# A conv block on one core: ScalarE's tap products and copies moved behind the job's sigmoid, ten VectorE taps moved ahead, the last copies split eight and eight

## The chip, the core and the metric

One NeuronCore of a Trainium2 chip runs the whole kernel. The metric is device time in microseconds (us), the median of several runs. PE is TensorE (PEld its weight loads), DVE is VectorE, ACT is ScalarE, POOL is GpSimd, SP is SyncE, which issues the DMAs.

## The reference

One decoder layer on 256 tokens of width 2048, in float32. A modulation vector comes from `c`; then a convolution mixer; then an MLP:

```python
mod = silu(c) @ mod_w + mod_b                      # sh1, sc1, g1, sh2, sc2, g2
h = rms_norm(x, norm1_g) * (1 + sc1) + sh1
u = h @ w_in + b_in                                # 2048 -> 4096
a, gt = split(u, 2)
u = a * sigmoid(gt)                                # the gate
u = depthwise_causal_conv(u, dw_w, width=31) + dw_b
u = silu(layer_norm(u, ln_g, ln_b))
x = x + (1 + g1) * (u @ w_out + b_out)
h = rms_norm(x, norm2_g) * (1 + sc2) + sh2
x = x + (1 + g2) * (square(relu(h @ w1)) @ w2)     # 2048 -> 8192 -> 2048
```

## The kernel before, in words

Channels lie on the 128 partitions, so a 2048-wide activation is 16 tiles of 128 x 256 tokens. A float32 weight is split into a high half `hi` (a copy by ScalarE, L209) and a low half `lo` (a subtraction, L213, by GpSimd for the input projection), and three matmul products (L234 to L239) stand for one float32 product. Weights arrive by DMA in 1 MB buffers named `raw`, seven of them; a buffer is loaded again when its `lo` has been made.

The change lies in the middle of the kernel. The input projection with its gates is a list of 16 jobs `("in", n)`. The first eight are summed together before 137 us; jobs 8 to 15 follow one after the other, up to about 272 us. Job n computes the two tiles (value and gate half) of channel tile n. Around each job stand, in the order in which the program says them:

- the weight splits of job n+1 (`splits`);
- in jobs 8 to 12 `shared_taps`: tile 7 is convolved by ScalarE and GpSimd together. ScalarE makes 2 or 7 products of a shifted tile with a tap's weight (L700, L703), GpSimd adds them up (L705);
- `copy_wide`: sixteen small copies (32 partitions x 284) that lay a gated tile out for a convolution on TensorE (L779 on ScalarE, L777 on DVE). `COPY_AT` says at which job which tile is copied;
- the job's matmuls;
- the evacuation: `evac` (L536 on ScalarE, L537 on DVE) adds the two halves of the sum, `gate` makes the sigmoid (L817, ScalarE) and the gated product `u` (L819, DVE);
- for seven tiles the convolution on TensorE itself (`pe_conv`, matmuls of L802), evacuated by ScalarE (L810); then modulation rows (matmuls of L328), which fill TensorE's time;
- `advance(n)`: a number of taps (L676, one 128 x 256 multiply-add each) of the eight tiles that DVE convolves, 31 taps a tile, joined by L679. `ADVANCE` says how many taps follow the gate of which job.

Behind the tiles 0 and 1 a mean is found (L428 on TensorE, L737), and subtracted from the convolved tiles as a shift (L741, on GpSimd L855); sums and sums of squares follow by L747 (squares by L480, L946). Job 15's gate is the last one: its tile 15 is copied at once, by DVE and ScalarE together, and convolved on TensorE, and layer norm, SiLU and the output projection hang on it.

A scheduler puts each engine's instructions in order by the order of the program and by priority: `urgent()` moves what stands in it ahead by 400 places, and `issue_after(x)` keeps an instruction behind `x`. Within an engine the order is then fixed. PSUM tiles named `mm` exist twice; jobs and TensorE convolutions take them in turn, so a matmul may have to wait for an evacuation two tiles before it.

Of the kernel before, what the change touches and what calls it, by code (L numbers as in the profile page):

```python
# [11 lines left out]
ALU = mybir.AluOpType  # L12
# [5 lines left out]
KT = D // P  # L18
# [25 lines left out]
CONV_AT = {9: (0,), 10: (1,), 11: (9,), 12: (10,), 14: (12,), 15: (14,)}  # L44
POOL_TILE = 7
POOL_TAPS = {8: 2, 9: 7, 10: 7, 11: 7, 12: 7}
ADVANCE = {7: 41, 8: 10, 9: 45, 10: 45, 11: 38, 12: 24, 13: 24, 14: 99}
SHIFT = 2
COPY_AT = {8: 0, 9: 1, 10: 9, 11: 10, 13: 12}
PADDING = 752  # L50
# [6 lines left out]
HELD = 8  # L57
# [11 lines left out]
def conv_block(ctx: ExitStack, tc: tile.TileContext, x, vec, dwq, c_row, mod_r, mod_c, w_first, w_in, w_out, w1, w2, out):  # L69
    nc = tc.nc  # L70
# [15 lines left out]
    def col(name, j=0, n=1):  # L86
        at = VEC[name] + j
        return v[:, at : at + n]
# [31 lines left out]
    state = {"used": 0}  # L120
# [12 lines left out]
    def urgent():  # L133
        return tc.high_priority(offset=URGENT)
# [315 lines left out]
    def two():  # L450
        return tmp.tile([P, 2, T], F32, name="two", bufs=6)
# [44 lines left out]
    for job in jobs:  # L496
        n = quota.get(job, 0)
# [3 lines left out]
        if job[:2] in LATE_GATE:  # L501
            n = LATE_GATE[job[:2]][job[2]]
# [22 lines left out]
    def splits(job):  # L525
        for c in range(2):
            if job + (c,) in parts_early:
                continue
            on_pool = job[0] == "in" or job in POOLED
            with urgent():  # L530
                split_w(job + (c,), nc.gpsimd if on_pool else nc.vector)

    def evac(p, cs=slice(0, 2), out=None):
        t1 = two()[:, cs, :]
        t2 = two()[:, cs, :] if out is None else out
        nc.scalar.activation(t1, p[:, cs, T : 2 * T], AF.Copy)  # L536
        nc.vector.tensor_tensor(t2, p[:, cs, 0:T], t1, op=ALU.add)  # L537
        return t2
# [4 lines left out]
    for k2 in range(HALF):  # L543
# [5 lines left out]
        for j in range(2):  # L549
            g = (2 * k2 + j) % 4  # L550
# [68 lines left out]
    for k in range(KT):  # L619
# [4 lines left out]
        if c == 0:  # L624
            n = two()
# [30 lines left out]
    def cv(k):  # L656
        return cvs[k // 4][:, k % 4, :]
# [6 lines left out]
    def tap_of(ct, j):  # L664
        return u[ct][:, j : j + T], col("dww", ct * TAPS + j)
# [27 lines left out]
    def shared_taps(n):  # L693
        at, total = POOL_TILE, cv(POOL_TILE)
        slots = [cvs[3][:, m, :] for m in range(4)] + [cv(11)]
        slots += [cp.tile([P, T], F32, name="part", bufs=2) for _ in range(n - len(slots))]
        with urgent(), tc.issue_after(state["w_hi"]), tc.issue_after(state["pool"]):
            if n == POOL_TAPS[HELD]:
                s, w = tap_of(at, 0)
                nc.scalar.activation(total, s, AF.Identity, scale=w, bias=col("dwb", at))  # L700
            for part in slots[:n]:
                s, w = tap_of(at, next(taken_taps))
                state["part"] = nc.scalar.activation(part, s, AF.Copy, scale=w).ins  # L703
            for part in slots[:n]:
                state["part_sum"] = nc.gpsimd.tensor_tensor(total, total, part, op=ALU.add).ins  # L705
# [21 lines left out]
    def advance(n):  # L727
        for _ in range(n):
            next(conv_taps, None)
# [9 lines left out]
    def add_shift(tiles, n):  # L739
        by = state["small"][:, None, T : 2 * T].to_broadcast([P, n, T])  # L740
        return nc.vector.tensor_tensor(tiles, tiles, by, op=ALU.add).ins  # L741
# [28 lines left out]
    def copy_wide(ct, both=True):  # L770
        wides[ct] = cp.tile([P, 4, T + 28], F32, name="wide", bufs=2)
        for q in range(4):
            for g in range(4):
                dst = wides[ct][32 * q : 32 * q + 32, g, :]
                src = u[ct][32 * g : 32 * g + 32, q : q + T + 28]
                if both and (g % 2 or (q, g) == (3, 2)):
                    nc.vector.tensor_copy(dst, src)  # L777
                else:
                    nc.scalar.activation(dst, src, AF.Copy)  # L779
# [35 lines left out]
    def gate(i, t2):  # L815
        sg = two()[:, 0, :]
        state["sg"] = nc.scalar.activation(sg, t2[:, 1, :], AF.Sigmoid, bias=col("b_in", KT + i))  # L817
        u[i] = ubufs[i % len(ubufs)]
        state["gated"] = nc.vector.scalar_tensor_tensor(  # L819
            u[i][:, PAD : PAD + T], t2[:, 0, :], col("b_in", i), sg, op0=ALU.add, op1=ALU.mult  # L820
        ).ins
        return sg
# [6 lines left out]
    with urgent():  # L829
# [10 lines left out]
        gate(7, held[7])  # L840
    advance(ADVANCE[HELD - 1])

    for n, job in enumerate(jobs):
# [5 lines left out]
            taken = [(key, take(key)) for key in cols_in]  # L849
        if n < len(jobs) - 1:  # L850
            splits(jobs[n + 1])
        if n in POOL_TAPS:
            shared_taps(POOL_TAPS[n])
        if n == KT - 3:
            nc.gpsimd.tensor_tensor(cv(POOL_TILE), cv(POOL_TILE), state["shift"], op=ALU.add)  # L855
        if n in COPY_AT:
            with tc.issue_after(state["sg"].ins) if n == HELD else ExitStack():
                copy_wide(COPY_AT[n], False)
        if n == KT - 1:
            for key in parts_early:  # L860
# [43 lines left out]
        if kind == "in":  # L904
            with urgent():
                gate(i, evac(p, out=p[:, :, 0:T]) if i < KT - 1 else p[:, :, 0:T])
                if i >= KT - 2:
                    copy_wide(i, i == KT - 1)
            if n == KT - 4:
                add_shift(cvs[0], 4)  # L910
                add_shift(cvs[1][:, 0:3, :], 3)
# [15 lines left out]
            with tc.issue_after(state["gated"]):  # L927
                advance(ADVANCE.get(n, 0))
            if n == KT - 2:
# [162 lines left out]
        else:  # L1092
# [13 lines left out]
            for t, cs, p in sums.pop((kind, i // 2)):  # L1106
# [9 lines left out]
                else:  # L1116
                    g = two().rearrange("p a t -> p (a t)")[:, cs]
# [62 lines left out]
```

## Time and profile before

| | |
|---|---|
| time, median of 3 runs | 1098.15 us (1098.1 to 1098.56) |
| the profiled execution's own time | 1097.87 us |
| its span | 1096.1 us, 15367 instructions |
| granted TensorE clock | 0.997 |
| busy over the span | PE 1078.0 us (98%), DVE 747.5 (68%), ACT 520.2 (47%), POOL 217.2 (20%) |
| moved by DMA | 314.20 MB, mean 287 GB/s |

The span runs from the first to the last instruction of the trace; the time has a little more around it. A row of a timeline gives start and length in us, the engine, the line, what is written and read, and in brackets the idle time ahead of it with what ended it; "x16" merges sixteen instructions. One matmul instruction can show as several records, so their number is not that of the program's matmuls.

### The profile page before, as it was taken

To read this page: it belongs to the slowest core of one execution; us is meant where nothing else is said; L and a number is where in the kernel's file an instruction comes from. 1 tells how busy PE (TensorE), PEld (TensorE's weight loads), DVE (VectorE), ACT (ScalarE), POOL (GpSimd) and SP (SyncE) were. 2 spreads that over 40 slices of the span, in tenths; PEclk is the share of its full clock that TensorE was granted. 3 is DMA by queue.
4 is the path that set the end of the run, shared out by engine and by line. 5 is a ranking of instruction groups with operands and counts; after the bars stand their busy time and mean duration, and the time that the engine had idled before them with its cause. 6 is when DMAs were issued, how large, how long until landed. Compare 5 with 4: busy or idle time off the path is not lost.

```text
span 1096.1 us, 15367 instructions
## 1 busy us (share of the span) xinstructions
PE 1078.0 (98%) x5970; PEld 890.6 (81%) x5970; DVE 747.5 (68%) x1020; ACT 520.2 (47%) x705; POOL 217.2 (20%) x149
## 2 busy tenths in 40 slices
PE   6999999999999999999999999999999999999998
PEld 3888875778599988888888888888888888888887
DVE  5777889978667877787855677545566665565653
ACT  4111398666685686444444444333444333444431
POOL 0000179979589261000000000000000000000000
PEclk8999999999999999999999999999999999999999
DMA  9999998985999967899977899657887877788611
GB/s 382 420 421 420 414 416 304 375 331 227 381 397 399 369 261 242 267 314 346 399 272 202 246 262 317 240 133 296 251 240 236 227 213 213 232 247 238 213 66 39
DMA packets 142314, 314.20 MB, mean 287 GB/s; under 512 B 87585, under 2 KB 105505, under 8 KB 107297
## 3 DMA queue, kind: packets, MB, share of 16 engines
q1 hardware_dynamic: 142096, 313.10, 81.2%
q8 instruction: 47, 0.77, 0.3%
q14 instruction: 25, 0.20, 0.1%
q10 hardware_dynamic: 146, 0.13, 0.0%
HBM read 301.13 MB, written 12.07 MB: 286 GB/s over the span
## 4 chain that ended last, share of the span: by engine, by line
PE 82%; DMA 10%; ACT 3%; DVE 3%; issue 1%; DVEq 0%; SPq 0%
PE mm L276 20%; PE mm L275 20%; PE mm L277 20%; DMA raw<-mod_c 7%; PE mm L238 5%; PE acc L235 2%; PE acc L234 2%; PE acc L236 2%; PE mm L239 2%; DMA first<-w_first 2%; PE row L328 1%; DVE raw L408 1%; PE mm L802 1%; ACT wide L779 1%; DMA raw<-w_in 1%; ACT hi L209 1%
## 5 line engine op out<-in xcount | busy, mean ns | idle before, releaser
L209 ACT ACTIVATE hi<-raw 128x1024 fp32r<-128x1024 f32 x320 | 335.7, 1058 | 361.5 <-PE mm L277 330.2
L213 DVE TENSOR_TENSOR lo<-raw,hi 128x1024 fp32r<-128x1024 f32 x257 | 312.3, 1220 | 182.8 <-ACT hi L209 179.2
L276 PE MATMUL mm<-lo,u 128*128 128x512 f32 x496 | 193.0, 389 | 0.0
L275 PE MATMUL mm<-hi,u 128*128 128x512 f32 x496 | 193.0, 389 | 0.0
L277 PE MATMUL mm<-hi,u 128*128 128x512 f32 x496 | 192.9, 389 | 0.0
L277 PE MATMUL mm<-hi,hl 128*128 128x512 f32 x480 | 186.7, 389 | 0.0
L276 PE MATMUL mm<-lo,hl 128*128 128x512 f32 x480 | 186.7, 389 | 0.0
L275 PE MATMUL mm<-hi,hl 128*128 128x512 f32 x480 | 186.7, 389 | 0.0
L213 POOL TENSOR_TENSOR lo<-raw,hi 128x1024 fp32r<-128x1024 f32 x63 | 156.1, 2508 | 37.0 <-ACT hi L209 37.0
L408 DVE SCALAR_TENSOR_TENSOR raw<-raw,cond 128x2048 f32<-128x2048 f32 x50 | 118.0, 2362 | 38.0 <-DMA raw<-mod_c 38.0
L277 PEld LDWEIGHTS mm<-hi,u 128*128 128x128 f32 x496 | 93.1, 188 | 19.3
L276 PEld LDWEIGHTS mm<-lo,u 128*128 128x128 f32 x496 | 93.2, 188 | 19.0
L275 PEld LDWEIGHTS mm<-hi,u 128*128 128x128 f32 x496 | 93.1, 188 | 19.0
L277 PEld LDWEIGHTS mm<-hi,hl 128*128 128x128 f32 x480 | 90.1, 188 | 18.7
L275 PEld LDWEIGHTS mm<-hi,hl 128*128 128x128 f32 x480 | 90.1, 188 | 18.7
L276 PEld LDWEIGHTS mm<-lo,hl 128*128 128x128 f32 x480 | 90.1, 188 | 18.6
L676 DVE SCALAR_TENSOR_TENSOR acc<-u,v,acc 128x256 f32<-128x256 f32 x224 | 94.0, 485 | 1.2
L238 PE MATMUL mm<-hl,hi 128*128 128x512 f32 x224 | 79.8, 400 | 0.9 <-DVE u L819 0.9
L580 PE MATMUL mm<-two,first 128*128 128x256 f32 x240 | 57.3, 394 | 8.0 <-ACT two L638 8.0
L234 PE MATMUL acc<-hl,hi 128*128 128x256 f32 x224 | 63.4, 283 | 0.0
L235 PE MATMUL acc<-hl,hi 128*128 128x256 f32 x224 | 63.4, 283 | 0.0
L236 PE MATMUL acc<-hl,lo 128*128 128x256 f32 x224 | 63.4, 283 | 0.0
(218 smaller groups left out, 1288.4 us busy)
## 6 DMA issues: line engine op xcount, KB each, us to landing
raw<-w SPq DMA_DIRECT2D x128, 1024.0 KB, 5.4
raw<-mod_c SPq DMA_DIRECT2D x62, 1024.0 KB, 11.0
raw<-mod_r SPq DMA_DIRECT2D x32, 1024.0 KB, 8.7
raw<-w_in SPq DMA_DIRECT2D x16, 1024.0 KB, 10.6
raw<-w_out SPq DMA_DIRECT2D x16, 1024.0 KB, 7.8
first<-w_first SPq DMA_DIRECT2D x15, 1024.0 KB, 19.8
flat<-two SPq DMA_DIRECT2D x30, 256.0 KB, 2.6
two<-flat SPq DMA_DIRECT2D x120, 64.0 KB, 4.2
```

Source lines behind the costliest of these rows:

```text
L209: state["w_hi"] = nc.scalar.activation(hi, w[:, ks, :], AF.Copy).ins
L213: end = by.tensor_tensor(lo, w[:, ks, :], hi.bitcast(F32), op=ALU.subtract)
L234: nc.tensor.matmul(out_p, w, m[:, 0:T], start=begin, stop=False)
L235: nc.tensor.matmul(out_p, w, m[:, T : 2 * T], start=False, stop=False)
L236: state["mm_end"] = nc.tensor.matmul(out_p, lo[:, k % HALF, :], m[:, 0:T], start=False, stop=end)
L238: nc.tensor.matmul(p[:, c, :], hi[:, k % HALF, :], m, start=(k == 0), stop=(k == KT - 1))
L275: nc.tensor.matmul(p, p_hi, hi, start=begin, stop=False)
L276: nc.tensor.matmul(p, p_hi, lo, start=False, stop=False)
L277: nc.tensor.matmul(p, p_lo, hi, start=False, stop=end)
L408: nc.vector.scalar_tensor_tensor(w, w, 1.0, cb, op0=ALU.mult, op1=ALU.mult, accum_out=acc)
L580: step = nc.tensor.matmul(held[n][:, c, :], w[:, 2 * n + c, :], h, start=k == 0 and c == 0, stop=k == KT - 1, skip_group_check=True)
L676: nc.vector.scalar_tensor_tensor(out, s, w, acc, op0=ALU.mult, op1=ALU.add)
```

## The change

The tap products of `shared_taps` are named in the program behind the job's gate instead of ahead of its matmuls, and are kept behind that job's sigmoid; so is GpSimd's shift of tile 7, now at job 12 (as before, in effect: it stood ahead of job 13's matmuls). Each set of copies is kept behind the last sigmoid before it, at all jobs and not at job 8 alone. `ADVANCE` moves taps between jobs, above all ten more behind job 12's gate, so ahead of job 13's; the sum stays within the 31 taps of each tile. Of the last sixteen copies DVE makes eight instead of nine.

```diff
-ADVANCE = {7: 41, 8: 10, 9: 45, 10: 45, 11: 38, 12: 24, 13: 24, 14: 99}
+ADVANCE = {7: 41, 8: 10, 9: 44, 10: 47, 11: 39, 12: 34, 13: 24, 14: 99}
@@ shared_taps
-        with urgent(), tc.issue_after(state["w_hi"]), tc.issue_after(state["pool"]):
+        with urgent(), tc.issue_after(state["sg"].ins), tc.issue_after(state["pool"]):
@@ copy_wide
-                if both and (g % 2 or (q, g) == (3, 2)):
+                if both and g % 2:
@@ the loop over the jobs, ahead of the matmuls
-        if n in POOL_TAPS:
-            shared_taps(POOL_TAPS[n])
-        if n == KT - 3:
-            nc.gpsimd.tensor_tensor(cv(POOL_TILE), cv(POOL_TILE), state["shift"], op=ALU.add)
         if n in COPY_AT:
-            with tc.issue_after(state["sg"].ins) if n == HELD else ExitStack():
+            with tc.issue_after(state["sg"].ins):
                 copy_wide(COPY_AT[n], False)
@@ the same loop, behind the gate
                 if i >= KT - 2:
                     copy_wide(i, i == KT - 1)
+            if n in POOL_TAPS:
+                shared_taps(POOL_TAPS[n])
+            if n == KT - 4:
+                nc.gpsimd.tensor_tensor(cv(POOL_TILE), cv(POOL_TILE), state["shift"], op=ALU.add)
```

In the built programs the instructions of each engine are the same but for one copy that changes engines. ScalarE's order changes from job 8 to job 13: the order now runs add, sigmoid, products, TensorE convolution's evacuation, copies, weight splits. DVE's order changes at job 8 (add and gate earlier by six and ten taps) and from job 12 on (tile 11's taps all end ahead of job 13's gate or right behind it; two taps, the last product and the join that stood between the modulation column L408 and job 15's gate now stand ahead of L408). TensorE's column sum of the mean and its sums of squares move behind four matmuls of the next or the running job. GpSimd's order is the same up to job 15.

## The prediction

> **What bounds the kernel now.** I read the page first, then the waits of TensorE in the stretch that the change touches (130 to 300 us), then each engine's timeline around the waits found, and the order of instructions of both kernels, engine by engine.
>
> ```profile
> span 1096.1 us, 15367 instructions
> ...
> PE 82%; DMA 10%; ACT 3%; DVE 3%; issue 1%; DVEq 0%; SPq 0%
> ```
>
> The chain that ended last is TensorE for 82% of the span. Before 130 us it waits on DMA; behind that it is nearly all matmuls. So the change, whose edits lie between 147 and 285 us, can only win what TensorE waits there, and lose what it is made to wait. The waits of TensorE from 130 to 300 us:
>
> ```profile
> PE acc L802 <- DVE wide L777: 1.2, 1, 1.2
> PE mm L238 <- DVE u L819: 0.9, 1, 0.9
> ```
>
> There are two, 1.2 and 0.9 us; each is told below by its own row. No DMA is in this list, so transfers arrive in time here.
>
> **The wait at job 10 (0.87 us).** TensorE's rows, the last of job 8, the last of job 9 and the first of job 10:
>
> ```profile
> 147.75 2.78 PE L328 MATMUL row<-raw,cz 128*32 128x512 f32 x24
> 165.44 3.62 PE L328 MATMUL row<-raw,cz 128*32 128x512 f32 x32
> 169.93 0.47 PE L238 MATMUL mm<-hl,hi 128*128 128x512 f32 x1 [0.87 <-DVE u L819]
> ```
>
> Job 10 could start when the modulation rows end, 165.44 + 3.62 = 169.06; it starts at 169.93 because its PSUM buffer is freed by job 9's gate product (L819 on DVE). That gate hangs on ScalarE, which is a solid row of work:
>
> ```profile
> 149.76 1.99 ACT L209 ACTIVATE hi<-raw 128x1024 fp32r<-128x1024 f32 x2
> 151.66 0.59 ACT L700 ACTIVATE cv<-u,v 128x256 f32<-128x256 f32 x1
> 152.15 0.89 ACT L703 ACTIVATE cv<-u,v 128x256 f32<-128x256 f32 x2
> 153.07 2.25 ACT L779 ACTIVATE wide<-u 32x284 f32<-32x284 f32 x5
> 155.34 0.60 ACT L536 ACTIVATE two<-mm 128x512 f32<-128x512 f32 x1
> 155.96 4.49 ACT L779 ACTIVATE wide<-u 32x284 f32<-32x284 f32 x10
> 160.48 0.47 ACT L817 ACTIVATE two<-mm,v 128x256 f32<-128x256 f32 x1
> 160.85 3.89 ACT L209 ACTIVATE hi<-raw 128x1024 fp32r<-128x1024 f32 x4
> 164.64 2.10 ACT L703 ACTIVATE cv<-u,v 128x256 f32<-128x256 f32 x5
> 166.64 0.90 ACT L703 ACTIVATE part<-u,v 128x256 f32<-128x256 f32 x2
> 167.44 0.58 ACT L536 ACTIVATE two<-mm 128x512 f32<-128x512 f32 x1
> 168.78 0.47 ACT L817 ACTIVATE two<-mm,v 128x256 f32<-128x256 f32 x1 [0.77 <-DVE mm L537]
> ```
>
> and on DVE (job 9's low-half add L537 and gate product L819, the taps behind them, and L537 of job 10):
>
> ```profile
> 168.05 0.70 DVE L537 TENSOR_TENSOR mm<-mm,two 128x512 f32<-128x512 f32 x1 [0.76 <-ACT two L536]
> 169.29 0.48 DVE L819 SCALAR_TENSOR_TENSOR u<-mm,v,two 128x256 f32<-128x256 f32 x1 [0.54 <-ACT two L817]
> 169.69 10.27 DVE L676 SCALAR_TENSOR_TENSOR acc<-u,v,acc 128x256 f32<-128x256 f32 x26
> 186.52 0.69 DVE L537 TENSOR_TENSOR mm<-mm,two 128x512 f32<-128x512 f32 x1
> ```
>
> No row of ScalarE from 149.76 to 167.44 shows an idle time before it, so this queue, not TensorE, sets when job 9's evacuation (L536) begins: 167.44. The change takes work out of the way. First, all sixteen copies of tile 1 now stand behind job 8's sigmoid, where one stood ahead of the weight splits at 149.76; a copy costs 2.25/5 = 0.45, so the splits begin at 149.31 and end at 149.31 + (151.66 - 149.76) = 151.21. Second, L536 of job 8 follows at once: its sum was complete by 147.75, when the next matmuls began. From L536 to the sigmoid L817 takes 168.78 - 167.44 = 1.34 (DVE's add lies between), the sigmoid 160.85 - 160.48 = 0.37: done at 152.92. DVE's add is not late either: the new order puts it six taps further ahead, and in the trace DVE stands idle for ScalarE here (the gate of 169.29 follows the sigmoid of 168.78 directly). Third, three tap products, 153.07 - 151.66 = 1.41, until 154.33; sixteen copies, 7.2, until 161.53; four splits, 164.64 - 160.85 = 3.79, until 165.32. Fourth, the seven tap products of job 9 (167.44 - 164.64 = 2.80) now come behind the sigmoid, so L536 starts at 165.3 instead of 167.44: 2.1 earlier, the 2.80 less the time that ScalarE now idles between job 8's L536 and its sigmoid, which ten copies covered before. The gate product then ends at 169.29 + 0.48 - 2.1 = 167.65, 1.4 before 169.06. The wait of **0.87** goes; TensorE's own rows are next. If ScalarE came out over 1.4 later than this, the gain would shrink by the excess.
>
> **What the moved tap products push back.** Behind the sigmoid they stand ahead of the evacuation of the tap convolution on TensorE (L810), of the next tile's copies, and of the next job's splits. The only early reader is the column sum (L428) that finds the shift, behind job 10:
>
> ```profile
> 187.25 0.47 ACT L817 ACTIVATE two<-mm,v 128x256 f32<-128x256 f32 x1 [3.02 <-DVE mm L537]
> 187.62 0.47 ACT L810 ACTIVATE cv<-mm,v 128x256 f32<-128x256 f32 x1
> ```
>
> ```profile
> 188.98 0.70 PE L428 MATMUL small<-cv,ones 128*128 128x256 f32 x2
> 189.60 1.05 PE L328 MATMUL row<-raw,cz 128*32 128x512 f32 x2
> ```
>
> DVE works without an idle row from 169.69 to 186.52, so if job 9's gate comes 2.1 earlier, L537 of job 10 comes at 184.4. The sigmoid starts 168.78 - 168.05 = 0.73 later (185.15), ends at 185.5, seven products 2.80 until 188.3, L810 0.47 until 188.8. TensorE, 0.87 earlier, reaches the second column sum at 188.98 - 0.87 + 1.05 (the last row chunk, which now stands ahead of it) = 189.2, and four matmuls of job 11 that the new order puts before it are a reserve on top. So it waits nothing, with a margin of 0.4 and more; I take **0**, bounded above by 1.7: without any lead on DVE, L810 ends at 187.62 + 0.47 + 2.80 = 190.9 against 189.2. The weight splits of job 11 come about 0.8 later on ScalarE (seven products 2.80 later, 2.1 earlier), those of jobs 12 to 14 similarly; each pair is wanted on TensorE only after a half job, several us, so this is hidden. GpSimd's sums and the loads on SP's queue that wait for the released weight buffers follow by the same 0.8; GpSimd's own order differs only by the line number of the shift, and later by one square sum; two loads of the output weights and two rows change places on SP. No wait of TensorE on DMA stands in the list above, so 0, and if that cover were gone, 0.8 once.
>
> **The ten taps ahead.** They go where DVE was idle:
>
> ```profile
> 242.31 0.70 DVE L537 TENSOR_TENSOR mm<-mm,two 128x512 f32<-128x512 f32 x1 [5.57 <-ACT two L536]
> 257.30 9.41 DVE L676 SCALAR_TENSOR_TENSOR acc<-u,v,acc 128x256 f32<-128x256 f32 x18
> 267.58 0.42 DVE L741 TENSOR_TENSOR cv<-cv,small 128x256 f32<-128x256 f32 x1 [0.88 <-PE small L747]
> 267.92 3.72 DVE L408 SCALAR_TENSOR_TENSOR raw<-raw,cond 128x2048 f32<-128x2048 f32 x1
> 273.48 0.47 DVE L819 SCALAR_TENSOR_TENSOR u<-mm,v,two 128x256 f32<-128x256 f32 x1
> ```
>
> Its first row has 5.57 us of idle time before job 13's add. Ten taps alone, without a second tile between, take 9.41/18 = 0.52 each (second row): 5.2. They fit, and what they clear are the four DVE operations between the modulation product L408 (ends 267.92 + 3.72 = 271.64) and the last gate product at 273.48. The add itself may come a trace late; its tile is needed some 10 us on. Two lone taps now stand between job 14's add and its gate: 0.69 (the row of 186.52) + 1.05 = 1.74 against 1.24 (169.29 - 168.05), so that gate and all of ScalarE's work behind it come up to 0.5 later; TensorE's start of job 15 does not wait for a gate in the list above.
>
> **The tail, where the wait of 1.22 us is.** The last sigmoid, the shared lines of GpSimd's weight splits, the DVE copies and TensorE's convolution of tile 15:
>
> ```profile
> 272.73 0.46 ACT L817 ACTIVATE two<-mm,v 128x256 f32<-128x256 f32 x1
> ```
>
> ```profile
> 267.08 2.41 POOL L213 TENSOR_TENSOR lo<-raw,hi 128x1024 fp32r<-128x1024 f32 x1 [2.10 <-ACT hi L209]
> 269.45 4.44 POOL L213 TENSOR_TENSOR lo<-raw,hi 128x1024 fp32r<-128x1024 f32 x1
> 276.19 2.44 POOL L213 TENSOR_TENSOR lo<-raw,hi 128x1024 fp32r<-128x1024 f32 x1
> ```
>
> ```profile
> L777 DVE COPY wide<-u x9: 298/301/2404, 274.0 to 280.7; 32x284 f32<-32x284 f32 x9
> ```
>
> ```profile
> 280.41 3.89 PE L802 MATMUL acc<-wide,diag 128*32 128x256 f32 x59 [1.22 <-DVE wide L777]
> ```
>
> TensorE waits for the copies. DVE's nine take 0.30 each, but up to 2.40: the first ones end when a GpSimd split ends (276.19 + 2.44 = 278.63 is the last), and the seven that are left then run at 0.3, up to some 281. L408 shows the same, 3.72 long because the split from 267.08 ran until 269.45; and that held the next split (4.44). The Trainium skill, in "SBUF — State Buffer", section Who interferes with whom, says that a VectorE copy in a two-port mode, or an operation with two SBUF inputs, and a GpSimd operation lock each other out for a whole instruction, first come first served, and that ScalarE never waits. The trace agrees with the blocking (2.40 against 0.30). By the rule's first come, first served, the copy that is issued ahead of the split at 273.9 passes before it, which would give the upper end of the tail below, and 1096.7; that lies inside the forecast's case.
>
> In rows: one copy fewer on DVE is 0.30 sooner at the end; the copy that ScalarE takes in its stead ends long before. Without the four operations (two taps, the last product, the join) behind L408 the gate product waits for the sigmoid alone: 272.73 + 0.46 = 273.2 instead of 273.48. The copies then start at 273.7, against 269.45 + 4.44 = 273.89 for the end of the second split: one copy may slip in between two splits and another 0.30 goes. L741 now waits for column sums that stand four matmuls later, but L408 behind it waits for the split until 269.45 anyway. Against this stands the 0.5 that ScalarE's queue, and with it the splits on GpSimd, may come later. So the tail is between 0.30 - 0.5 = -0.2 and 0.6 of gain; I take **0.2**, the middle, since both ends rest on races of a tenth.
>
> **Sum.** 0.87 + 0.2 = 1.07. The profiled execution has a span of 1096.1 in its own time of 1097.87, so about 1095.0 and 1096.8 after; the median of the runs is 1098.15, 0.28 above the profiled execution, which gives 1097.1.
>
> **Rivals.**
> The tail opens wholly: if GpSimd's four splits end before the copies start, TensorE loses neither the 1.22 nor the two steps of 0.3 of the last copies: 1098.15 - 0.87 - 1.8 = 1095.5; with the 1.22 alone 1096.1. Against it: the splits hang on ScalarE's rows behind sixteen copies, whose order is unchanged.
> The column sum takes the place of job 10's wait: if L810 behind the seven products ends after 189.2, TensorE waits there. At the upper bound of 1.7 the net is 0.8 lost, less 0.2 in the tail: 1098.8, slower than before. It decides from the point where DVE reaches job 10's add later than 184.8; for it speaks that the add waited 3.02 for DVE's queue of taps, against it that this queue begins with job 9's gate.
> The change does not gain: job 10's wait is replaced by one for the splits or for a row's load, 0.8, and the tail is even: 1098.1.
>
> **How the numbers follow.** The forecast has 0.62; the open tail 0.16 (half of it beyond 0.2%); the column sum 0.12; no gain 0.06; 0.04 for something slower than all of these, since every queue is shifted. A measurement of this kernel can tell about 0.2% (2.2 us) from no change: faster means under 1095.95, slower over 1100.35. Faster 0.12: half of the open tail and a little of the forecast with a better tail; slower 0.07; same 0.81. The range runs from 1095.6, into the open tail, to 1098.7, nearly the whole price of the column sum.
>
> **What would show it.** In the trace after: no wait of L238 on L819 at job 10; L536 of job 9 near 165.3; L428 with no wait on L810; DVE idle before job 13's add nearly gone; two or three copies of 2.4 and the rest of 0.3; TensorE's last convolution resuming 1.0 to 1.5 earlier than 280.41, and the same distance kept to the end. I am wrong if job 10 still waits, if ScalarE's row is not the limit at 165 us, or if TensorE waits at a place that has none now.

## The result, and the profile after

| | before | after |
|---|---|---|
| time, median of 14 runs each | 1098.09 us (1097.87 to 1098.56) | 1095.73 us (1095.45 to 1096.22) |
| span of the profiled execution | 1096.1 us | 1093.8 us |
| TensorE's waits from 130 to 300 us | 0.87 (job 10) and 1.22 (tail) | 1.26 (tail) |

The ratio is 0.9979, with a 95% interval of 0.9971 to 0.9987. The kernel is 2.36 us faster. The time lies in the predicted range, at its lower end, and 1.4 us under the predicted 1097.1. The median is also under the 1095.95 from which the prediction counts "faster", but the interval reaches to both sides of that line (0.998), so whether the gain exceeds 0.2% is not settled. The question is where another 1.3 us came from.

The list of TensorE's waits from 130 to 300 us, of after. Job 10's is gone:

```profile
PE acc L802 <- DVE wide L777: 1.3, 1, 1.3
```

**Job 10.** ScalarE's timeline of after, the weight splits ahead of job 9's evacuation, that evacuation, and the evacuation of tile 1's TensorE convolution:

```profile
161.65 3.90 ACT L209 ACTIVATE hi<-raw 128x1024 fp32r<-128x1024 f32 x4
165.46 0.58 ACT L536 ACTIVATE two<-mm 128x512 f32<-128x512 f32 x1
...
188.43 0.46 ACT L810 ACTIVATE cv<-mm,v 128x256 f32<-128x256 f32 x1
```

Job 9's evacuation L536 starts at 165.46 (167.44 before). DVE and TensorE behind it:

```profile
167.31 0.48 DVE L819 SCALAR_TENSOR_TENSOR u<-mm,v,two 128x256 f32<-128x256 f32 x1 [0.54 <-ACT two L817]
...
184.54 0.69 DVE L537 TENSOR_TENSOR mm<-mm,two 128x512 f32<-128x512 f32 x1
```

```profile
165.55 3.62 PE L328 MATMUL row<-raw,cz 128*32 128x512 f32 x32
169.10 0.50 PE L238 MATMUL mm<-hl,hi 128*128 128x512 f32 x1
```

Job 10 follows the rows at once, at 169.10 instead of 169.93: 0.83.

**The rows behind job 10.** TensorE's timeline between job 10 and job 11, of before:

```profile
181.19 3.66 PE L802 MATMUL mm<-wide,diag 128*32 128x256 f32 x64
184.78 0.70 PE L428 MATMUL small<-cv,ones 128*128 128x256 f32 x2
185.41 3.63 PE L328 MATMUL row<-raw,cz 128*32 128x512 f32 x30
...
190.58 0.50 PE L238 MATMUL mm<-hl,hi 128*128 128x512 f32 x1
```

and of after:

```profile
180.60 3.66 PE L802 MATMUL mm<-wide,diag 128*32 128x256 f32 x64
184.19 0.70 PE L428 MATMUL small<-cv,ones 128*128 128x256 f32 x2
184.82 3.64 PE L328 MATMUL row<-raw,cz 128*32 128x512 f32 x32
188.39 0.50 PE L238 MATMUL mm<-hl,hi 128*128 128x512 f32 x1
...
189.07 0.28 PE L239 MATMUL mm<-hl,lo 128*128 128x256 f32 x1
189.19 0.59 PE L428 MATMUL small<-cv,ones 128*128 128x256 f32 x2
...
189.86 0.28 PE L239 MATMUL mm<-hl,lo 128*128 128x256 f32 x1
```

A row matmul shows as two records, so x30 is fifteen matmuls and x32 is sixteen, which the program issues in four chunks of four. Fifteen took 3.63 us, sixteen take 3.64. The sixteenth, which in the kernel before stood alone behind the column sum (189.60, 1.05 long, 0.98 until job 11 starts), costs nothing beside the others. From the first column sum to job 11 it was 190.58 - 184.78 = 5.80; now it is 188.39 - 184.19 = 4.20, and the second sum costs 0.43 inside job 11 (from one L239 to the next 189.86 - 189.07 = 0.79, where two L239 usually lie 0.36 apart). So 5.80 - 4.20 - 0.43 = 1.17 came from here, a place where the prediction had 0.

**The tail.** DVE, GpSimd and TensorE of after; the copies' row is from the view of one tile:

```profile
271.55 0.48 DVE L819 SCALAR_TENSOR_TENSOR u<-mm,v,two 128x256 f32<-128x256 f32 x1 [1.30 <-ACT two L817]
```

```profile
L777 DVE COPY wide<-u x8: 299/304/2411, 272.1 to 278.8; 32x284 f32<-32x284 f32 x8
```

```profile
265.69 11.62 POOL L213 TENSOR_TENSOR lo<-raw,hi 128x1024 fp32r<-128x1024 f32 x4 [2.59 <-ACT hi L209]
```

```profile
278.79 1.49 PE L802 MATMUL acc<-wide,diag 128*32 128x256 f32 x20 [1.26 <-DVE wide L777]
```

The wait is still there. GpSimd's four splits end at 265.69 + 11.62 = 277.31, and the last copy starts at 278.8. TensorE resumes at 278.79 instead of 280.41, 1.62 earlier.

**The account on TensorE**, by the start of the same matmul in both kernels: 0.83 earlier at job 10, 0.59 at its end (181.19 to 180.60: the job itself took 11.50 us instead of 11.26), 0.59 + 1.17 = 1.76 behind the rows, about 1.7 in jobs 12 to 15, 1.95 from the tail to the last matmul. The span is 2.24 shorter and the median 2.36: some 0.3 lies behind the last matmul (see the last part).

### The profile page after: what moved, and what is told of

Its sections match the earlier page's. It is cut to its first block, busy times and chain, and to the rows that moved or that the text cites. A ratio compares the mean times of both kernels' runs of the same rounds, so it can differ in the third digit from the quotient of the medians.

```text
span 1093.8 us, 15366 instructions
## 1 busy us (share of the span) xinstructions
PE 1075.9 (98%) x5970; PEld 889.9 (81%) x5970; DVE 748.5 (68%) x1019; ACT 520.1 (48%) x706; POOL 217.4 (20%) x149
## 4 chain that ended last, share of the span: by engine, by line
PE 86%; DMA 10%; DVE 3%; ACT 1%; issue 0%; SPq 0%; ACTq 0%
PE mm L276 20%; PE mm L275 20%; PE mm L277 20%; DMA raw<-mod_c 9%; PE mm L238 6%; PE mm L239 3%; PE acc L235 2%; PE acc L234 2%; PE acc L236 2%; PE row L328 2%; PE mm L802 2%; DVE raw L408 1%; DMA x<-x 1%; DVE wide L777 1%; PE mm L234 0%; PE mm L236 0%
## 5 line engine op out<-in xcount | busy, mean ns | idle before, releaser
L408 DVE SCALAR_TENSOR_TENSOR raw<-raw,cond 128x2048 f32<-128x2048 f32 x50 | 117.8, 2358 | 40.5 <-DMA raw<-mod_c 40.5
```

Source lines behind the costliest of these rows:

```text
L408: nc.vector.scalar_tensor_tensor(w, w, 1.0, cb, op0=ALU.mult, op1=ALU.mult, accum_out=acc)
```

## The experiments

Most of the edits undo or make one part of the change, in before or in after; the last three change the tail of after further. Medians of before stood at 1098.05 to 1098.12 beside all of them. Each effect is about a tenth of a per cent, and so is the distance from a ratio to either end of its 95% interval, so the trace decides and the median only has to agree.

**The cut group of four.** `mod_chunk` issues its four row matmuls to the four groups of 32 output columns (`row_ps[0][32 * k : 32 * k + 32]`). The first theory: four such matmuls run side by side, so one that is cut off takes the time of four. In before, the column sum (`find_shift`) is put elsewhere, first behind all the rows, then behind twelve of them; `shift_end` is the sum's last matmul:

```diff
# b_sum_behind
         pe_conv(ct)
-        if ct == SHIFT - 1:
-            find_shift()
...
                     mods(rows)
+                if ct == SHIFT - 1:
+                    with tc.issue_after(state["row_end"].ins):
+                        find_shift()
```

> The kernel before, with one thing changed: the two matmuls of tile 1's column sum (L428) are put behind all sixteen row matmuls of job 10, where they stood between the fifteenth and the sixteenth... Theory (four row matmuls use the four groups of 32 columns at the same time, and the sixteenth, cut off from its group of four, cost a whole slot of 0.98 us): 0.9 to 1.0 us less than before, about 1097.1; the sixteen rows take about 3.64 us together, as the fifteen did. Rival (the last row costs its time wherever it stands, as the prediction had it): 0, and sixteen rows of about 4.6 us. The wait of 0.87 at job 10 stays in both.

```diff
# b_sum_at_four (find_shift taken out of mix, as above)
-                    mods(rows)
+                    mods(rows[:-1])
+                if ct == SHIFT - 1:
+                    with tc.issue_after(state["row_end"].ins):
+                        find_shift()
+                with tc.issue_after(state["shift_end"].ins) if ct == SHIFT - 1 else ExitStack():
+                    mods(rows[-1:])
```

> The kernel before, with the column sum's two matmuls behind the twelfth of job 10's row matmuls, a boundary of four, so that they still stand ahead of the last rows. Theory (what cost 0.98 us is a group of four that was cut): about as much less as with the sum behind all sixteen, 0.7 to 1.0 us under the kernel before; a small wait for L810 (it ended at 188.09, and twelve rows end at about 188.1) may take 0.1 of it. Rival (what counts is that the sum stands ahead of rows at all, which drain TensorE's pipeline once): 0, within 0.2 of the kernel before.

TensorE's timeline, of the kernel with the sum behind all rows:

```profile
184.98 3.62 PE L328 MATMUL row<-raw,cz 128*32 128x512 f32 x32
188.53 1.13 PE L428 MATMUL small<-cv,ones 128*128 128x256 f32 x4
189.31 0.58 PE L238 MATMUL mm<-hl,hi 128*128 128x512 f32 x1
```

and with the sum at a boundary of four:

```profile
185.00 2.76 PE L328 MATMUL row<-raw,cz 128*32 128x512 f32 x24
187.69 1.28 PE L428 MATMUL small<-cv,ones 128*128 128x256 f32 x4
188.90 1.06 PE L328 MATMUL row<-raw,cz 128*32 128x512 f32 x8
189.90 0.50 PE L238 MATMUL mm<-hl,hi 128*128 128x512 f32 x1
```

The medians are 1096.66 (1.4 under before; ratio 0.9987, 0.9978 to 0.9996) and 1097.23 (0.8 under; 0.9992, 0.9984 to 1.0001; its slowest run, 1097.47, is under the fastest of before, 1097.84). Sixteen rows take 188.53 - 184.98 = 3.55, and the last four 189.90 - 188.90 = 1.00, as much as the lone one. So the rival that only standing ahead of rows costs is out: here the sum does stand ahead of rows, and the whole stretch is 189.90 - 185.00 = 4.90 against 5.80. The first kernel gained more than was expected, because both pairs of the sum side by side cost 0.78 (188.53 to 189.31) where two separate ones cost 0.63 each. In the second kernel they cost 188.90 - 187.69 = 1.21 side by side, because the weights of the second pair waited 0.3 for L810; without that it would have gained more too.

That the four run side by side can also be read from single records, which the rows above merge. In before, the last whole group starts its four first records at 187.153 to 187.173 and its four second ones at 187.582 to 187.602, 0.43 us later. The cut group starts three at 188.011 to 188.024 and three at 188.440 to 188.454, so three take the two steps of 0.43 that four take. The lone matmul's two records start at 189.605 and 190.059: it has two steps of 0.45 and 0.52 for itself.

The reverse, in after: the first pair of the sum, which waits for nothing, is put between the fifteenth and the sixteenth row matmul.

```diff
# a_sum_cut, in mod_chunk, for the last chunk behind job 10
         for k in range(4):
+            if k == 3 and state.pop("cut", False):
+                with tc.issue_after(state["row_end"].ins):
+                    ...
+                    state["first_sum"] = nc.tensor.matmul(state["small"][:, 0:T], ones, cv(0), start=True, stop=False)
```

> The kernel after, with one thing put back in another form: the first matmul of the column sum, that of tile 0, which is ready long before, is put between the fifteenth and the sixteenth row matmul of job 10, where the kernel before had the second one. Nothing waits for it. Theory (the sixteenth row matmul, cut off from its group of four, costs a slot of its own): 0.9 to 1.1 us over after, about 1096.7, and fifteen rows take as long as sixteen. Rival (the gain of after over its prediction came from something else, the second sum's place behind L810 or the pace of job 10's matmuls): within 0.3 of after.

```profile
183.94 3.61 PE L332 MATMUL row<-raw,cz 128*32 128x512 f32 x30
187.48 0.70 PE L331 MATMUL small<-cv,ones 128*128 128x256 f32 x2
188.11 1.05 PE L332 MATMUL row<-raw,cz 128*32 128x512 f32 x2
189.09 0.50 PE L238 MATMUL mm<-hl,hi 128*128 128x512 f32 x1
```

The lone row is back, with its 0.98 (188.11 to 189.09), and the stretch is 189.09 - 183.94 = 5.15 instead of 4.20: 0.95, as the theory has it. Of this only 0.55 shows in the median (1096.28), less than expected: TensorE came 0.25 earlier to the stretch in this execution (0.13 of it before the convolution ahead of the stretch began), and 0.2 of the delay went again inside job 11. The place is shown, the size at the end is uncertain by these 0.3.

**The products at job 10.** In after, the seven tap products of job 9 go back ahead of its evacuation; TensorE's order stays that of after.

```diff
# a_taps9_front
+        if n == 9:
+            shared_taps(POOL_TAPS[n], state["w_hi"])
         if n in COPY_AT:
...
-            if n in POOL_TAPS:
+            if n in POOL_TAPS and n != 9:
```

> The kernel after, with job 9's seven tap products of tile 7 back ahead of job 9's evacuation on ScalarE; TensorE's order is that of after, so the column sum keeps its new place. Theory (the products' place set job 10's wait): L536 of job 9 starts 2.8 us later than in after, at about 168.3, and TensorE waits 1.4 to 1.7 us at job 10 (longer than the 0.87 of before, since two splits fewer stand behind them); the time is 1.2 to 1.7 us over after. Rival (the gain came from the column sum alone, and job 10's start is made up behind it): under 0.4 over after.

From 130 to 300 us TensorE now waits three times: 1.26 in the tail, as in after, and at two other places that the rows of ScalarE and TensorE show:

```profile
168.15 0.57 ACT L536 ACTIVATE two<-mm 128x512 f32<-128x512 f32 x1
187.96 0.47 ACT L817 ACTIVATE two<-mm,v 128x256 f32<-128x256 f32 x1 [5.16 <-DVE mm L537]
191.12 0.46 ACT L810 ACTIVATE cv<-mm,v 128x256 f32<-128x256 f32 x1
```

```profile
170.63 0.47 PE L238 MATMUL mm<-hl,hi 128*128 128x512 f32 x1 [1.57 <-DVE u L819]
191.63 0.70 PE L428 MATMUL small<-cv,ones 128*128 128x256 f32 x2 [0.78 <-ACT cv L810]
```

The median is 1098.26, that is 2.5 over after: more than expected, because a second wait comes, and the two together are 2.35. The seven products alone set when job 10 can start: L536 at 168.15 instead of 165.46, and 1.57 of wait. And the prediction's slower rival appears: job 10's sigmoid waits for DVE's add, the products behind it push L810 to 191.12 (188.43 in after), and the column sum waits 0.78. So the change holds only as a whole: with job 10's products behind the sigmoid and job 9's ahead, it is no faster than before.

**The tail's parts.** The number of DVE's copies alone, both ways, and the taps alone, both ways.

```diff
# b_eight in before; a_nine the reverse in after
-                if both and (g % 2 or (q, g) == (3, 2)):
+                if both and g % 2:
# b_advance in before; a_advance the reverse in after
-ADVANCE = {7: 41, 8: 10, 9: 45, 10: 45, 11: 38, 12: 24, 13: 24, 14: 99}
+ADVANCE = {7: 41, 8: 10, 9: 44, 10: 47, 11: 39, 12: 34, 13: 24, 14: 99}
```

> The kernel before, with the last sixteen copies shared eight and eight instead of nine on VectorE and seven on ScalarE; nothing else. Theory (one VectorE copy of 0.30 us is off the end of the chain, and ScalarE's is hidden): 0.3 us less, TensorE's last convolution (L802) resumes at about 280.1 instead of 280.4. Rival (the copies end with GpSimd's splits, which does not depend on their number): 0.

> The kernel after, with nine of the last sixteen copies on VectorE, as before. Theory: 0.3 us over after, L802 resumes at 279.1 instead of 278.8. Rival (the splits set the end): 0.

> The kernel before, with only the numbers by which VectorE's taps are put ahead changed to those of after. Theory (the ten taps fill idle time ahead of job 13 and clear four operations in front of the last gate product, so one copy can slip in ahead of a split): 0 to 0.3 us less than before; the idle time ahead of job 13's add falls from 5.57 to under 1; the first VectorE copy begins 0.2 to 0.3 earlier. Rival (the later gate of job 14 pushes ScalarE's splits and GpSimd's back as far): 0 to 0.3 more. TensorE's wait at job 10 (0.87) and the cut group of rows stay.

> The kernel after, with the numbers of before by which VectorE's taps are put ahead (ten taps back behind job 13). Theory (the taps ahead let the first of the last copies slip in before a split): 0.2 to 0.4 us over after, and VectorE idle for 5 us again ahead of job 13's add. Rival (they stand beside other work and change nothing): 0 to 0.1.

The last column is what TensorE's start times shift from job 15 to behind the tail, against the base's trace:

| | median | against its base | shift in the tail |
|---|---|---|---|
| b_eight | 1097.57 | -0.5 | 0.34 earlier |
| a_nine | 1096.09 | +0.4 | 0.33 later |
| b_advance | 1097.84 | -0.2 | 0.02 later |
| a_advance | 1095.58 | -0.15 | 0.03 earlier |

One copy fewer on DVE is worth 0.3: both directions agree. The ten taps are worth nothing in the tail, in either direction, against the theory of both expectations. Of after without them, GpSimd's row:

```profile
265.21 11.55 POOL L213 TENSOR_TENSOR lo<-raw,hi 128x1024 fp32r<-128x1024 f32 x4 [2.14 <-ACT hi L209]
```

The splits begin 0.48 earlier (265.21 against 265.69; 0.2 of it TensorE had already, in all jobs behind job 10), although DVE stands idle ahead of job 13's add again and the last gate product follows four DVE operations again. So in after the two lone taps between job 14's add and its gate push ScalarE's splits, and GpSimd's behind them, back by 0.3, as much as the earlier copies gain. That gain is one copy: in after the first, at 272.07, takes 0.58 and slips in between the second split and the third, and five are left when the last split ends; without the ten taps the first is held for 2.42, and six are left. The prediction had both, the slipped copy in its upper end with 0.30 and the later splits in its lower end with 0.5.

**What makes the wait of 1.26.** Two edits in after. The first takes two of the four splits away from the copies:

```diff
# a_late_part
-        if n == KT - 1:
-            for key in parts_early:
-                split_w(key, nc.gpsimd)
... behind the last copies:
+            if n == KT - 1:
+                for key in parts_early:
+                    with tc.issue_after(state["copied"]):      # ScalarE's last copy
+                        split_w(key, nc.gpsimd)
```

> The kernel after, with GpSimd's and ScalarE's early split of an output weight block moved behind ScalarE's last copies, so that only two GpSimd splits stand beside VectorE's last copies instead of four. Theory (TensorE's last wait of 1.26 us is made by copies that are held for whole splits of 2.4 us): copies of 0.3 us throughout, L802 without a wait on a copy of over 0.3, 1.3 to 1.8 us under after, about 1094.1. Rival (the split is then late for the output projection, which waits for it in turn): 0 or above.

The view of the copies' tile, and of TensorE at the tail, where it now waits for nothing:

```profile
L777 DVE COPY wide<-u x8: 298/301/1404, 271.3 to 274.6; 32x284 f32<-32x284 f32 x8
```

```profile
276.93 2.37 PE L802 MATMUL acc<-wide,diag 128*32 128x256 f32 x40
```

The tail opens as the theory said: DVE's last copy starts at 274.6 instead of 278.8, and TensorE is 1.9 earlier from there to 373 us. But the time is 1098.18, 2.4 over after. The next lines are TensorE's waits behind 300 us, where after has none, and its granted clock (the column PEclk) in that stretch:

```profile
PE acc L234 <- ACT hi L209: 1.6, 1, 1.6
PE acc L236 <- DVE lo L213: 0.8, 1, 0.8
```

```profile
core 0: us, PE busy (x), PEclk, DMA share, GB/s
...
373.00:376.00 3.00, 0.64 (x4) 1.00 0.40 167
376.00:378.00 2.00, 2.00 (x12) 0.65 0.16 25
378.00:380.00 2.00, 2.00 (x12) 0.50 0.84 291
380.00:382.00 2.00, 2.00 (x19) 1.00 0.90 279
```

The scheduler, with the split elsewhere, puts ScalarE's split of a late output weight behind an activation that waits for TensorE, 90 us on; the rival had named another weight but the same kind of loss. And the loss is more than the waits: behind them the clock stands at half for some 3.5 us. Of the 4.35 us lost there, 2.4 are the two waits and about 1.5 the slow matmuls (18 starts in 3.65 us from 376.56 to 380.21, where they take 0.12 each otherwise); the other 0.5 lies in the matmuls right beside the waits. In the Trainium skill, "TensorE: Matmul & The Clock Gate", section What's actually happening, a window of about 3.4 us without work halves the clock until a busy one follows. The trace agrees with the half (0.50) and, for the time at half clock, with the length; it adds that 0.64 us of work in 3.00 did not keep the clock up. Three of the eleven runs took only 1096.8, some 1.4 less than the others, about what the slow matmuls cost; whether the clock stayed up in them is not shown, because the trace is of another run. Their times too are above those of after.

That one order was then fixed (the activation is kept behind the split by `issue_after`):

> The kernel with the early output split behind ScalarE's last copies, which opened the tail by 1.96 us and then lost 4.4 at 374 us, where ScalarE's split of the last output weight had come to stand behind the residual's activation (L1030) that waits for TensorE. Here that activation is ordered behind the split again. Theory (the 4.4 us are this one order and TensorE's lower clock behind it): no wait at 374 us, 1.7 to 2.0 us under after, about 1093.9. Rival (the weight itself comes later when the split ahead of it does, or the orders that shift in the up projection make a new wait): at or above after's 1095.7.

```profile
PE row L356 <- ACT rowsb L354: 2.4, 1, 2.4
```

The wait at 374 is gone and another of 2.4 stands at 400 us, in the up projection, where the scheduler had moved more: ScalarE's copy L354 stands behind an activation that waits for DVE until 399.55. Here too the loss, from 2.1 earlier than after to 3.5 later, is more than the wait: the granted clock is 0.50 from 401 to 407 us. The median is 1098.76 (1097.18 to 1100.58). The rival holds; ordering that one place did not make moving the split pay.

The second edit leaves GpSimd alone and gives ScalarE twelve of the sixteen copies:

```diff
# a_twelve
-                if both and g % 2:
+                if both and g == 1:
```

> The kernel after, with the last sixteen copies shared twelve on ScalarE and four on VectorE. In after VectorE's eight end at about 278.8 because two of them are held for whole GpSimd splits (2.4 us each, the last split ends at 277.3), while ScalarE's eight, 0.45 each, end at 275.7 and ScalarE then waits. Theory (only VectorE's copies are held, and what follows the last split is 0.3 for each copy left): ScalarE's twelve end at 272.07 + 12 x 0.45 = 277.5, VectorE's four at about 277.9; TensorE's convolution resumes 0.8 to 1.0 earlier than 278.79, the wait of 1.26 falls to about 0.4, and the time is 0.8 to 1.0 under after, about 1094.8. Rival (ScalarE's copies are held as well once they stand beside the splits, or something else ends at 278.8): 0 or above.

```profile
271.95 5.40 ACT L779 ACTIVATE wide<-u 32x284 f32<-32x284 f32 x12 [0.55 <-DVE u L819]
```

```profile
271.95 5.70 DVE L777 COPY wide<-u 32x284 f32<-32x284 f32 x4
```

```profile
277.70 3.44 PE L802 MATMUL acc<-wide,diag 128*32 128x256 f32 x59 [0.30 <-DVE wide L777]
```

The median is 1094.83 (ratio to before 0.9973, 0.9964 to 0.9982), 0.9 under after, as the theory had it, by one condition in the code. Ten of its eleven runs lie at 1094.67 to 1094.97, under the fastest of after (1095.45); one took 1098.77, and why is not known. ScalarE's copies take 5.40/12 = 0.45 each beside the same splits that hold DVE's: the four of DVE take 5.70, the longest 2.40. The Trainium skill says in "SBUF — State Buffer", section Who interferes with whom, that at the SBUF ports ScalarE never waits on another engine, and that a VectorE copy in a two-port mode and GpSimd block each other. The trace agrees with both, with 0.45 and 2.40.

## Why the prediction was right or wrong

- **The wait at job 10** (0.87): right, step by step. L536 of job 9 at 165.46 (165.3 predicted), DVE's add of job 10 at 184.54 (184.4), the gain 0.83 at the start of job 10. That its cause is the place of the products is shown by the kernel that puts job 9's back. Of the 0.83, 0.24 went again inside job 10, which took longer. It need not be the change's: in the kernel that differs from before in one copy at 274 us job 10 took 11.47 (169.92 to 181.39) instead of 11.26, too. Such differences of 0.2 between executions bound what a single trace can say here.
- **The column sum, 0**: this is the term that was mis-sized. That it does not wait was right (L810 ends at 188.89, 188.8 predicted). But the step "188.98 - 0.87 + 1.05" took the 1.05 of what it calls the last row chunk as work that only changes places. It was not a chunk but the last matmul of one, and the 1.05 was the cost of its place. The rows that stood in the prediction had it: 32 records in 3.62 are 0.11 each, so two of them should have taken 0.2 and not 1.05. The stretch is worth 1.17, more than the whole forecast. The same slip took away the margin of 0.4: the rows were done by 188.39, not 189.2, ahead of L810's end at 188.89. The column sum did not wait because of the four matmuls of job 11 ahead of it, which the prediction named only as a reserve; it began at 189.19.
- **The tail, 0.2**: 0.30 measured, and the kind was right. One copy is 0.3, and what the taps gain and lose cancels. The four operations ahead of the last gate are cleared, as said; the gate product now waits for the sigmoid, and the tail gains nothing by it. TensorE resumes 1.62 earlier, just outside the 1.0 to 1.5 that was named as a sign.
- **The sum**: 1.07 forecast; on TensorE 0.83 - 0.24 + 1.17 = 1.76, of which jobs 11 to 15 give back 0.1 and the tail adds 0.3: 1.95. The rest up to 2.24 of the span lies behind the last landing. That the range holds 1095.73 is luck: its lower end, 1095.6, was set for a tail that opens, and the time came there by the column sum.
- **The rivals**: the tail did not open (1.26 against 1.22). What would open it was the number of copies behind the splits, on which a_twelve acts. The column sum as a wait did not come in after, and came as described, 0.78, when job 9's gate was late. Job 10's wait was not replaced by one for the splits or a row's load: the list of waits has none.

## What to carry to other kernels

Before a matmul is priced from its own row, compare it with the rate of its neighbours of the same form: a record that takes five times its share is paying for where it stands, and the next change of order will give or take that. Where an engine's small operations are held by another's long ones, count how many are left when the last long one ends, and hand the rest to an engine that isn't held, rather than start earlier. An order that a scheduler finds can turn a local gain into a stall a hundred microseconds on, so read the waits of the whole span.

## What was not expected of the hardware

- A row matmul into one group of 32 columns, alone between full-width matmuls, takes 0.98 us; four of them to four groups take 1.00.
- Two waits of TensorE of 1.6 and 0.76 us with little work between cost another 1.5 us at half clock, and one of 2.4 us was followed by half clock as well. The single waits of 0.87, 1.26 and 1.57 left the granted clock at 1.00.
- From the last landing of a DMA to the end of the span it is 1.44 us in before (1094.65 to 1096.09) and 1.15 in after (1092.70 to 1093.85). It was 1.44 in the two kernels that only move the column sum in before, and 1.15 to 1.22 in all others measured, those with one copy or the taps changed in before among them. What sets it stays open; it is 0.3 of the 2.36, and the 0.5 of b_eight holds 0.2 of it.
